# Cutting GpSimd's last store unevenly instead of SyncE's store of four earlier heads

## Chip, core and metric

The kernel runs on one core of one Trainium2 chip. The metric is the device time of one execution in microseconds (us), as the median of several runs.

## What is computed

Attention over 8 x 12 = 96 heads of 512 positions and 64 channels. The positions are the nodes of a binary tree in heap order, and a query sees only itself and its ancestors.

```python
mask = np.zeros((seq, seq))
for i in range(seq):
    mask[i, i] = 1
    parent = i
    while parent > 0:
        parent = (parent - 1) // 2
        mask[i, parent] = 1
scores = np.einsum('bhqd,bhkd->bhqk', Q, K) * scale
scores = scores + (1 - mask) * (-1e9)
weights = np.exp(scores - np.max(scores, axis=-1, keepdims=True))
weights = weights / (np.sum(weights, axis=-1, keepdims=True) + 1e-10)
return np.einsum('bhqk,bhkd->bhqd', weights, V).astype(np.float32)
```

## The kernel before

The 96 heads are worked in 48 pairs (NP = 48). The main loop runs over i = 0 to 48. Step i computes the scores of pair i on TensorE (`scores1`, `scores2`), takes their exponentials on ScalarE, multiplies the weights of pair i - 1 with V (`values`) and divides by the row sums on VectorE (`norm`, L691 and L693). `turn` transposes the keys and queries of later pairs. Loads of Q, K and V are issued from GpSimd, which converts them from f32 to bf16 on the way; GpSimd also copies pieces of V and of Q and K into place (L370, L444).

`norm` writes into output tiles `of` of eight heads each, 128 partitions x 8 heads x 256 floats. From pair 16 on, `head(i, a)` is 8 * (i // 4) + i % 4 + 4 * a: four pairs fill one tile, and pair i writes head x and head x + 4. So heads 76 and 77 are finished by pair 37, heads 78 and 79 by pair 39, heads 72 to 79 all by pair 39, and heads 80 to 87 by pair 43. Heads 88 to 95 are filled by the last four pairs.

`store(eng, h0, n, step, p0, p1)` (L700 to L706) writes n heads of one tile from the partitions p0 to p1 to the output. One head is 128 KB, 1 KB in each partition. An issue from GpSimd goes through the software queue (q0 in the profile), one from SyncE or ScalarE through a hardware queue (q1, q10). The order on GpSimd is a written list (`pool_program`, L717 to L763) whose operations are taken in order when `ready` allows; each then waits on chip for its data. Its stores are issued like this: heads 0 to 39 in the loop over loads, then 40 to 47, and so on by eight up to 80 to 87, with one exception: the store at 72 takes only four heads. The other four of that tile are stored by SyncE in `store_apart` (L711 to L715), called after step 41: heads 76 and 77 in two DMAs of partitions 0 to 59 and 60 to 127, heads 78 and 79 in one. SyncE stores 88 and 92, 89 and 93, 90 and 94 in pairs as they are finished (L890), then 91 (L892), and ScalarE stores 95 (L893).

The tiles are separate for each eight heads, and there are eleven buffers (NOUT // 2) for the twelve of them.

Of the kernel before, what the change touches and what calls it, by code (L numbers as in the profile page):

```python
# [119 lines left out]
def kernel(  # L120
# [7 lines left out]
    nc = tc.nc  # L128
    B, H, S, D = Q.shape
    P = nc.NUM_PARTITIONS  # L130
    assert S == 512 and D == 64 and P == 128 and (B * H) % 4 == 0
    scale = float(1.0 / np.sqrt(D))
    NH = B * H
# [3 lines left out]
    KB, VB = 8, 16  # L137
# [424 lines left out]
    def scores1(i):  # L562

        sp = psS.tile([P, 2, 512], fp32, name="s1")
        for a in range(2):
            nc.tensor.matmul(  # L566
                out=sp[:, a, :],
                lhsT=(k1code if i < WIDE else k1wide)[64 * a:64 * a + CODE_ROWS, :],
                rhs=(q1code, q1wide, q1far)[(i >= WIDE) + (i >= FAR)][64 * a:64 * a + CODE_ROWS],
                start=True, stop=False,  # L570
            )
        for a in range(2):
            nc.tensor.matmul(  # L573
                out=sp[:, a, :], lhsT=keys(i, a, TOP),
                rhs=qTs[i][64 * a:64 * a + 64, :, :].rearrange("p t c -> p (t c)"),
                start=False, stop=True,
            )
        et = etpool.tile([P, 2, 4, 128], bf16, name="e1")
        nc.scalar.activation(  # L579
            out=et[:, :, :, :].rearrange("p a t c -> p (a t c)"),  # L580
            in_=sp[:, :, :].rearrange("p a c -> p (a c)"),
            func=AF.Exp, scale=scale,
        ) if i < WIDE else nc.scalar.activation(  # L583
            out=et[:, :, :, :].rearrange("p a t (r u) -> p a (t r) u", u=2 if i < FAR else 4),
            in_=sp[:, :, :].rearrange("p a (u c) -> p a c u", u=2 if i < FAR else 4),
            func=AF.Exp, scale=scale,
        )
        ets[i] = et
# [34 lines left out]
    def scores2(i):  # L623
        if i >= WIDE:
            return scores2_wide(i)
        sp = psS.tile([P, 2, 4, 128], fp32, name="s2")
        flat = sp[:, :, :, :].rearrange("p a t c -> p a (t c)")
        for a in range(2):
            nc.tensor.matmul(
                out=sp[:, a, :, 32:128], lhsT=k2code[64 * a:64 * a + CODE_ROWS, :],  # L630
                rhs=q2code[64 * a:64 * a + CODE_ROWS, :].rearrange(
                    "p (t c) -> p t c", t=4
                )[:, :, 32:128],
                start=True, stop=False,
            )
        for t, lo, hi in ((2, 32, 192), (0, 192, 256), (3, 288, 448), (1, 448, 512)):
            for a in range(2):
                nc.tensor.matmul(
                    out=flat[:, a, lo:hi], lhsT=keys(i, a, TILE2[t]),
                    rhs=qTs[i][64 * a:64 * a + 64, :, :].rearrange("p t c -> p (t c)")[:, lo:hi],  # L640
                    start=False, stop=t == 1, skip_group_check=t in (2, 3),
                )
        nc.scalar.activation(
            out=e2s[i % NE][:, :, :, 32:128].rearrange("p a t c -> p (a t) c"),
            in_=sp[:, :, :, 32:128].rearrange("p a t c -> p (a t) c"),
            func=AF.Exp, scale=scale,
        )
# [52 lines left out]
    def store(eng, h0, n, step=1, p0=0, p1=P):  # L700
        return eng.dma_start(  # L701
            out=Or[p0:p1, h0:h0 + step * (n - 1) + 1:step, :],
            in_=ofs[h0 // 8][p0:p1, h0 % 8:h0 % 8 + step * (n - 1) + 1:step, :, :].rearrange(
                "p h t d -> p h (t d)"
            ),
        )  # L706


    APART, APART_AT, APART_ROWS = 76, 41, 60

    def store_apart():  # L711

        for p0, p1 in ((0, APART_ROWS), (APART_ROWS, P)):
            store(nc.sync, APART, 2, 1, p0, p1)
        store(nc.sync, APART + 2, 2)  # L715

    def pool_program():  # L717

        ops = [
            (load_k, 2, 2), (load_q, 2, 2), (load_v, 0, 4), (load_v, 4, 4),  # L720
            (load_k, 4, 2), (load_k, 6, 2), (load_q, 4, 2), (load_k, 8, 4),
            (load_q, 6, 2), (load_q, 8, 4), (load_v, 8, 8), (load_k, 12, 4),
            (load_q, 12, 4), (load_k, 16, 4), (load_rows, 1, "upper"),
            (load_q, 16, 4), (load_rows, 1, "even"), (load_k, 20, 4), (load_rows, 1, "odd"),
            (load_q, 20, 4), (load_k, 24, 8), (load_q, 24, 4), (load_rows, 2, "upper"),
            (load_q, 28, 4), (load_rows, 2, "leaves0", "leaves1"), (load_k, 32, 8), (load_q, 32, 8),
            (load_rows, 3, "upper"),
            (spread_pool, (1, "Z0", 8, 16), (1, "Z1", 8, 16), (1, 6, 8, 16), (1, 9, 8, 16)),
            (load_q, 40, 8), (load_k, 40, 8), (load_rows, 3, "leaves0", "leaves1"), (load_q, 48, 8),
            (spread_top, 2), (spread_pool, (2, "Z0", 0, 16), (2, "Z1", 0, 16)), (load_k, 48, 8),  # L730
            (spread_pool, (2, "X", 0, 16), (2, "M", 0, 16), (2, "D1", 0, 16)), (spread_top, 3, 0, 12),
            (load_rows, 4, "upper"), (spread_top, 3, 12, 16),
        ]
        loaded, stored = 72, 0
        for h in range(56, NH, KB):
            top = [(spread_top, h // VB + 0)] if h % VB == 8 and 4 <= h // VB + 0 < NH // VB else []
            if top:
                top.append((spread_pool, (h // VB, "Z0", 0, 16), (h // VB, "Z1", 0, 16)))
            ops += [(load_q, h, KB)] + top + [(load_k, h, KB)]
            if h == 64:  # L740
                ops.append((
                    spread_pool, *[(3, part, 0, 16) for part in ("Z0", "Z1", "X", "M", "D1")]
                ))
            while loaded < min(h + 32, NH):
                names = ("leaves0", "leaves1") if loaded % VB else ("upper",)
                ops.append((load_rows, loaded // VB) + names)
                loaded += KB
            if top:
                o = h // VB
                ops.append((spread_pool, *[(o, part, 0, 16) for part in ("X", "M", "D1")]))  # L750
            if stored + KB + BEHIND <= h + KB:
                ops.append((store, nc.gpsimd, stored, KB))
                stored += KB
        ops.append((lay_beside, "qst", 80 // KB))
        while stored < NH - KB:
            n = 4 if stored + 4 == APART else KB
            ops.append((store, nc.gpsimd, stored, n))
            if stored == 40:
                ops.append((lay_beside, "kst", 80 // KB))
            if stored == 64:  # L760
                ops += [(lay_beside, "qst", 88 // KB), (lay_beside, "kst", 88 // KB)]
            stored += KB
        return ops  # L763
# [58 lines left out]
    def spread_by(copy, table, steady, i):  # L822
# [7 lines left out]
        for args in todo:  # L830
            spread(copy, *args)

    program = pool_program()

    def pool(i):
# [21 lines left out]
    for i in range(NP + 1):  # L857
        steps = FIRST[i] if i < len(FIRST) else "SVK" if i % 2 else "SVQ"
        steps = "SQVK" if i == FAR - 1 else steps
        for step in steps:  # L860
            if step == "S" and i < NP:
                scores1(i)
                scores2(i)
            if step == "V" and i >= 1:
                values(i - 1)
                norm(i - 1)
                valued = True
            if step == "K" and kdone < NP:
                kdone = turn("kst", kdone)
            if step == "Q" and qdone < NP:  # L870
                qdone = turn("qst", qdone)
            if step == "W":
                nc.scalar.copy(
                    out=codes[64:64 + CODE_ROWS, 1280:1536], in_=codes[0:CODE_ROWS, 1280:1536]
                )
            if step == "X":
                spin("s1" if valued else "ob", 2)
            if step == "D":
                spread_by(nc.vector.tensor_copy, BY_VECTOR, STEADY_VECTOR, i)
            if step == "A":  # L880
                spread_by(nc.scalar.copy, BY_SCALAR, STEADY_SCALAR, i)
        if "D" not in steps:
            spread_by(nc.vector.tensor_copy, BY_VECTOR, STEADY_VECTOR, i)
        if "A" not in steps:
            spread_by(nc.scalar.copy, BY_SCALAR, STEADY_SCALAR, i)
        pool(i)
        if i == APART_AT:
            store_apart()
        if i >= NP - 3 and i < NP:
            store(nc.sync, head(i - 1, 0), 2, 4)  # L890
    assert not program
# [32 lines left out]
```

## Time and profile before

| | |
|---|---|
| runs | 133.47, 133.77, 133.95 us; median 133.77 |
| profiled execution, first to last instruction | 131.7 us |
| around that span, by the median | 2.07 us |
| granted TensorE clock, mean | 0.969 |
| busy: TensorE, VectorE, ScalarE, GpSimd | 113.8, 103.6, 101.0, 83.1 us |
| HBM read, written | 37.94 MB, 12.58 MB |
| GpSimd's store issues | 11, 9.9 us busy |

No time of the profiled execution apart from its span is given, so the span stands for it; the 2.07 us are what the runs' median has beyond it. Busy times are those of one execution. A DMA's time to landing goes from its issue to its last completion, so it holds the time that it stood in the queue. DMA shares are the time of all packets over that of 16 engines, and can exceed 1 where packets overlap.

### The profile page before, as it was taken

The page shows a single profiled execution, that of the slowest core. Times are in us where ns is not written, and L with a number is a line of the kernel's source. Part 1 is how long each engine was busy: PE and PEld are TensorE (multiplying, and loading weights), DVE is VectorE, ACT ScalarE, POOL GpSimd, SP SyncE. Part 2 cuts the span into 40 slices and gives each one's busy share as a digit, 9 for nine tenths or more (in the row PEclk, how much of TensorE's full clock was granted, in tenths as well). Part 3 has the DMA queues.
Part 4 walks back from the last instruction along what each step waited for, and adds up shares of the span by engine and source line. Part 5 has one row for each costly group of instructions (what it writes and reads, how often), then busy time and mean ns, then how long its engine had stood idle before and what let it go on. Part 6 is the DMA issues. An engine that isn't in the chain of part 4 may idle for free.

```text
span 131.7 us, 5422 instructions
## 1 busy us (share of the span) xinstructions
PE 113.8 (86%) x2350; PEld 79.8 (61%) x2353; DVE 103.6 (79%) x254; ACT 101.0 (77%) x163; POOL 83.1 (63%) x114
## 2 busy tenths in 40 slices
PE   6783999999899899999999998997998999999900
PEld 2341577676666567667676675765675777775600
DVE  3437849988999998989899879898899977975530
ACT  4357369979799997968997879895898878789800
POOL 6968734345493999895399899945999935002000
PEclk9999689999999999999999999999999999999975
DMA  2999999999999999999999999999999999999991
GB/s 98 239 181 194 198 198 200 202 202 206 204 200 212 205 203 208 211 205 204 207 207 201 301 275 204 285 290 234 339 218 332 241 288 402 402 398 392 397 350 64
DMA packets 28108, 32.25 MB, mean 245 GB/s; under 512 B 1165, under 2 KB 23309, under 8 KB 28085
## 3 DMA queue, kind: packets, MB, share of 16 engines
q0 software_dynamic: 25696, 29.63, 110.8%
q1 hardware_dynamic: 1829, 1.83, 3.9%
q10 hardware_dynamic: 560, 0.46, 1.2%
q8 instruction: 18, 0.29, 0.8%
q14 instruction: 5, 0.04, 0.1%
HBM read 37.94 MB, written 12.58 MB: 384 GB/s over the span
## 4 chain that ended last, share of the span: by engine, by line
DMA 30%; PE 30%; DVE 15%; POOL 9%; ACT 7%; issue 4%; ACTq 0%; POOLq 0%
DMA qst<-in_Q_dram 14%; DMA kst<-in_K_dram 11%; PE ob L661 10%; POOL vt L370 6%; DMA vst<-in_V_dram 5%; DVE of L693 5%; PE s L566 4%; DVE vt L370 3%; PE s L573 3%; ACT e L617 3%; PE s L600 2%; PE s L611 2%; ACT vt L370 2%; PE qtp L531 2%; PE ktp L469 2%
## 5 line engine op out<-in xcount | busy, mean ns | idle before, releaser
L583 ACT ACTIVATE e<-s 128x1024 bf16<-128x1024 f32 x40 | 40.9, 1022 | 13.0 <-PE s L573 12.7
L661 PE MATMUL ob<-vt,e 128*128 128x65 bf16 (+1 forms) x940 | 37.4, 198 | 1.5 <-DVE of L693 1.0
L661 PEld LDWEIGHTS <-e 128*128 128x128 bf16 (+1 forms) x960 | 30.5, 103 | 9.5 <-PE s L611 1.0
L370 POOL COPY vt<-vst 32x512 int32<-32x512 int32 (+4 forms) x44 | 32.6, 741 | 5.3 <-PE ob L661 3.1
L617 ACT ACTIVATE e<-s 128x384 bf16<-128x384 f32 x80 | 34.7, 490 | 0.0
L693 DVE TENSOR_TENSOR of<-ob,rec 128x512 f32<-128x512 f32 x47 | 32.5, 692 | 1.6
L370 DVE COPY vt<-vst 32x1024 bf16<-32x1024 bf16 (+5 forms) x47 | 21.4, 456 | 3.1 <-DMA vst<-in_V_dram 2.2
L691 DVE RECIPROCAL rec<-ob 128x8 f32<-128x8 f32 x47 | 9.6, 205 | 12.1 <-PE ob L661 11.2
L701 POOL DMA_DIRECT2D out_dram<-of x11 | 9.9, 898 | 8.9 <-DVE of L693 8.8
L573 PE MATMUL s<-qq,kq 64*128 64x512 bf16 x80 | 15.3, 377 | 0.0
L611 PE MATMUL s<-qq,kq 64*128 64x160 bf16 (+1 forms) x320 | 14.8, 208 | 0.3 <-issue 0.3
L611 PEld LDWEIGHTS <-kq 64*128 64x128 bf16 x320 | 12.3, 94 | 4.5 <-issue 0.5
L566 PE MATMUL s<-far,codes 40*128 40x512 bf16 x64 | 12.5, 386 | 0.1
L600 PEld LDWEIGHTS <-codes 40*128 40x128 bf16 x80 | 6.4, 95 | 10.1 <-issue 4.5
L579 ACT ACTIVATE e<-s 128x1024 bf16<-128x1024 f32 x8 | 8.2, 1022 | 5.2 <-PE s L573 5.2
L253 POOL DMA_DIRECT2D qst<-in_Q_dram x12 | 8.5, 708 | 5.5 <-DMA kst<-in_K_dram 3.1
L370 ACT COPY vt<-vst 32x512 int32<-32x512 int32 (+3 forms) x19 | 10.4, 545 | 2.1 <-DMA vst<-in_V_dram 1.6
L542 DVE COPY qq<-qtp 128x1024 bf16<-128x1024 bf16 x16 | 10.9, 682 | 0.8 <-PE qtp L537 0.8
L253 POOL DMA_DIRECT2D kst<-in_K_dram x11 | 8.4, 762 | 4.3 <-DMA vst<-in_V_dram 2.0
L600 PE MATMUL s<-far,codes 40*128 40x384 bf16 x64 | 10.6, 324 | 0.6 <-ACT e L617 0.5
L476 PE MATMUL ktp<-ptile,kst 128*64 128x128 bf16 x256 | 10.1, 220 | 0.9 <-DVE kq L493 0.3
L298 POOL DMA_DIRECT2D vst<-in_V_dram x7 | 5.6, 800 | 5.8 <-DMA vst<-in_V_dram 4.0
(56 smaller groups left out, 155.8 us busy)
## 6 DMA issues: line engine op xcount, KB each, us to landing
out_dram<-of POOLq DMA_DIRECT2D x10, 1024.0 KB, 15.7
kst<-in_K_dram POOLq DMA_DIRECT2D x9, 512.0 KB, 14.2
qst<-in_Q_dram POOLq DMA_DIRECT2D x8, 512.0 KB, 16.1
vst<-in_V_dram POOLq DMA_DIRECT2D x12, 256.0 KB, 13.2
vst<-in_V_dram POOLq DMA_DIRECT2D x6, 512.0 KB, 12.4
qst<-in_Q_dram POOLq DMA_DIRECT2D x6, 256.0 KB, 11.9
kst<-in_K_dram POOLq DMA_DIRECT2D x4, 256.0 KB, 9.6
out_dram<-of SPq DMA_DIRECT2D x4, 256.0 KB, 6.5
```

What stands on the lines that cost most here:

```text
L253: return nc.gpsimd.dma_start(out=kept[b][:, h0 % KB:h0 % KB + n, :, :].rearrange("p (g x) t d -> p g (x t d)", x=x), in_=src[:, h0 // x:(h ...
L370: return copy(out=dst, in_=src)
L476: nc.tensor.transpose(out=columns(kp[64 * a:64 * a + 64, :], mixed, *dims), in_=st[:, place[a], 4 * u + t, :], identity=ptile[:, 0:128],)
L542: nc.vector.tensor_copy(out=qqs[j][:, :, 8 * last:8 * last + 8, :].rearrange("p b u c -> p b (u c)"), in_=quarters,)
L566: nc.tensor.matmul(out=sp[:, a, :], lhsT=(k1code if i < WIDE else k1wide)[64 * a:64 * a + CODE_ROWS, :], rhs=(q1code, q1wide, q1far)[(i >= ...
L573: nc.tensor.matmul(out=sp[:, a, :], lhsT=keys(i, a, TOP), rhs=qTs[i][64 * a:64 * a + 64, :, :].rearrange("p t c -> p (t c)"), start=False, ...
L583: ) if i < WIDE else nc.scalar.activation(
L600: nc.tensor.matmul(out=flat[:, a, :, :].rearrange("p u (t c) -> p u t c", t=4)[:, :, :, 32 // n:], lhsT=k2wide[64 * a:64 * a + CODE_ROWS, ...
L611: nc.tensor.matmul(out=flat[:, a, :, lo:hi], lhsT=keys(i, a, WTILE2[t]), rhs=qT[64 * a:64 * a + 64, :, lo:hi], start=False, stop=t == 1, s ...
L617: nc.scalar.activation(out=e2s[i % NE][:, a, :, 32:128].rearrange("p t (r u) -> p t r u", u=n), in_=flat[:, a, :, :].rearrange("p u (t r) ...
L661: nc.tensor.matmul(out=ob[lo:hi, a, 65 * t:65 * t + 65], lhsT=e[:, a, PLACE[t], lo:hi], rhs=vt[vtile[tile_v][0]][:, head(i, a) % VB, vtile ...
L693: nc.vector.tensor_tensor(out=ofs[j][:, h0:h1 + 1:head(i, 1) - head(i, 0), :, :], in0=o4[:, a:a + n, :, 0:D], in1=rec[:, a:a + n, :, :].to ...
```

## The change

`store_apart` and its call are removed, and with them SyncE's DMAs for heads 76 to 79. The store at 72 loses its exception and takes all eight heads 72 to 79. The short description of the change says that heads 72 to 77 go in one DMA and heads 78 and 79 in two of 60 and 68 partitions. The code does this one tile later: its condition `stored + KB == NH - KB` is 80 + 8 == 96 - 8, so it is heads 80 to 85 that go in one DMA, and heads 86 and 87 in the two. In the built kernel GpSimd's last four DMAs are 128x8x256, 128x6x256, 60x2x256 and 68x2x256, the last three of one tile; before they ended with 128x4x256 and 128x8x256. GpSimd has two DMAs more, SyncE three fewer. The order on TensorE, VectorE and ScalarE is the same.

```diff
-    APART, APART_AT, APART_ROWS = 76, 41, 60
-
-    def store_apart():
-
-        for p0, p1 in ((0, APART_ROWS), (APART_ROWS, P)):
-            store(nc.sync, APART, 2, 1, p0, p1)
-        store(nc.sync, APART + 2, 2)
-
...
         while stored < NH - KB:
-            n = 4 if stored + 4 == APART else KB
-            ops.append((store, nc.gpsimd, stored, n))
+            if stored + KB == NH - KB:
+                ops.append((store, nc.gpsimd, stored, KB - 2))
+                for p0, p1 in ((0, 60), (60, P)):
+                    ops.append((store, nc.gpsimd, stored + KB - 2, 2, 1, p0, p1))
+            else:
+                ops.append((store, nc.gpsimd, stored, KB))
...
-        if i == APART_AT:
-            store_apart()
```

## The prediction

> **What bounds the kernel now.** I read the page's head and slices first, then busy time by windows over the last 22 us, then the DMA issues of that stretch one by one, then the waits at the end.
>
> ```profile
> span 131.7 us, 5422 instructions
> DMA  2999999999999999999999999999999999999991
> DMA 30%; PE 30%; DVE 15%; POOL 9%; ACT 7%; issue 4%; ACTq 0%; POOLq 0%
> ```
>
> The DMA engines are busy in every slice but the first and the last, and the chain that ended last spends as much in DMA as on TensorE. So the stores at the end do not run on an idle memory system: they stand in a backlog. The windows (columns: stretch, length, busy us of PE, PEld, DVE, ACT, POOL, granted clock, DMA share, GB/s) show that it lasts beyond the arithmetic:
>
> ```profile
> 110.00:114.00 4.00, 4.00 (x81) 2.95 (x79) 3.18 (x7) 3.22 (x6) 0.94 (x2) 1.00 1.04 400
> 114.00:118.00 4.00, 4.00 (x82) 3.04 (x76) 3.18 (x8) 3.23 (x7) 0.00 (x0) 1.00 1.03 400
> 118.00:122.00 4.00, 3.75 (x74) 2.45 (x70) 2.01 (x5) 3.83 (x7) 0.91 (x1) 1.00 1.01 394
> 122.00:126.00 4.00, 3.23 (x66) 2.16 (x62) 2.38 (x7) 2.75 (x6) 0.00 (x0) 1.00 1.00 384
> 126.00:130.00 4.00, 0.00 (x0) 0.00 (x0) 0.55 (x3) 0.00 (x0) 0.00 (x0) 0.63 0.74 264
> ```
>
> From 110 to 118 the DMA engines move 400 GB/s with a share over 1, and after 126, when TensorE has nothing left, they still move 4.00 us x 264 GB/s = 1.06 MB. At 400 GB/s that is 2.6 us. The store issues and their landings (KB, us from issue to landing) say what stands in that backlog; the timeline gives GpSimd's and SyncE's start times, the DMA view of a short window round each start gives the landing:
>
> ```profile
> 104.53 0.89 POOL L701 DMA_DIRECT2D out_dram<-of  x1
> out_dram<-of POOLq DMA_DIRECT2D x1, 1024.0 KB, 19.4
> 110.99 0.76 POOL L701 DMA_DIRECT2D out_dram<-of  x1 [0.82 <-DVE of L693]
> out_dram<-of POOLq DMA_DIRECT2D x1, 512.0 KB, 14.6
> 119.69 0.91 POOL L701 DMA_DIRECT2D out_dram<-of  x1 [7.94 <-DVE of L693]
> out_dram<-of POOLq DMA_DIRECT2D x1, 1024.0 KB, 8.7
> 121.54 0.39 SPq L701 DMA_DIRECT2D out_dram<-of  x1
> out_dram<-of SPq DMA_DIRECT2D x1, 256.0 KB, 7.1
> 125.27 1.14 SPq L701 DMA_DIRECT2D out_dram<-of  x2
> L701 SPq DMA_DIRECT2D out_dram<-of x7: 350/373/398, 106.4 to 126.1; - x7
> out_dram<-of SPq DMA_DIRECT2D x1, 128.0 KB, 4.2
> SPq L919 <- DMA out_dram<-of: 3.9, 5, 1.9
> ```
>
> GpSimd's store of 104.53 has landed whole at 123.9, that of 110.99 at 125.6, that of 119.69 (heads 80 to 87) at 128.4. SyncE's last store, the second of the pair that starts at 125.27, starts at 126.1 and lands at 130.3; at the end SyncE waits for stores (five waits, 3.9 us). So neither queue runs dry before about 128.4, and the kernel ends when the last of the 16 DMA engines has written its last row. The next row cuts 128.5 to 131 into 40 slices of 0.0625 us:
>
> ```profile
> GB/s 262 279 262 197 213 148 180 131 148 98 115 82 115 66 66 82 49 82 33 66 33 66 33 49 49 33 33 0 0 0 0 0 0 0 0 0 0 0 0 0
> ```
>
> The rate does not stop at once: it falls from 262 to 33 GB/s over 1.7 us. At 400 / 16 = 25 GB/s for one engine, about ten are still writing at 128.5 and one or two at 130.2. The engines are unevenly loaded and the slowest sets the end. What counts about this change is therefore not bytes in all, which stay the same, but bytes per DMA engine.
>
> **The change, part by part.** In the code the condition `stored + KB == NH - KB` holds at stored = 80. So GpSimd's store of heads 72 to 75 becomes one of all of 72 to 79, its store of 80 to 87 becomes one of 80 to 85, and heads 86 and 87 go in two DMAs of 60 and 68 partitions. SyncE's three DMAs for 76 to 79 go.
>
> *SyncE's three issues.* Removed, at
>
> ```profile
> 106.37 0.36 SPq L701 DMA_DIRECT2D out_dram<-of  x1
> 106.77 0.39 SPq L701 DMA_DIRECT2D out_dram<-of  x1
> 110.72 0.40 SPq L701 DMA_DIRECT2D out_dram<-of  x1
> SPq L701 <- DVE of L693: 11.7, 2, 10.4
> ```
>
> That is 1.15 us of a queue that then waits 10.4 us for VectorE: worth nothing. The bytes leave at 110.99 instead of 106.37 and 110.72, behind a software queue that is full until 123.9 anyway: nothing by itself.
>
> *GpSimd's two more issues.* One of its store issues takes
>
> ```profile
> L701 POOL DMA_DIRECT2D out_dram<-of x11: 763/912/962, 60.2 to 119.7; - x11
> ```
>
> so the 8-head store at 110.99 costs about 0.15 us more than the 4-head one, inside an idle 7.94 us. After 119.69 the six-head store and two small ones take at most 3 x 0.96 = 2.9 us: the last is queued by 122.6. The queue ahead of it is busy until 125.6, so 3 us of cover hide it. Without the cover it would cost up to 1.9 us. Nobody on GpSimd waits behind these.
>
> *Rows per engine.* This is the term with a price. How the hardware queue dealt the old uneven pair is seen in its packets (q1 is SyncE's, q0 GpSimd's; packets, MB, share), first in 116 to 117, then in 120 to 121:
>
> ```profile
> out_dram<-of SPq DMA_DIRECT2D x1, 120.0 KB, 7.4
> out_dram<-of SPq DMA_DIRECT2D x1, 136.0 KB
> out_dram<-of SPq DMA_DIRECT2D x1, 256.0 KB, 11.8
> q0 software_dynamic: 84, 0.31, 77.6%
> q1 hardware_dynamic: 85, 0.09, 24.6%
> q0 software_dynamic: 97, 0.38, 96.6%
> q1 hardware_dynamic: 21, 0.02, 6.0%
> ```
>
> In 116 to 117 the two queues alternate packet by packet (84 and 85). In 120 to 121 SyncE's queue moves a quarter of that, 21, until its 256 KB store lands at 122.5, 11.8 us after issue, where the next one took 7.1. A quarter of 16 engines is four: the 136 KB lay on four of them, 34 KB each, and held up what came behind. The 120 KB are 15 groups of four rows x 2 heads x 1 KB, 8 KB on an engine. So of the four heads 76, 77, 86 and 87, twelve engines wrote 8 + 16 = 24 KB and four wrote 58 KB. After the change 76 and 77 are even, 16 KB each; 86 and 87 are uneven in the software queue, which the trace of before never shows for such counts. At best 60 rows are 4 on each of 15 engines and 68 rows 5 on most, 18 KB in all. The twelve light engines then go from 24 to 34 KB: 10 KB at 25 GB/s, +0.41 us. The bounds of the light share are 16 KB before (+18 KB, 0.72 us) and 32 KB (+2 KB, 0.08 us); 24 is nearest to what the packets show. The four heavy ones lose 24 KB, 0.97 us.
>
> *Software packets for hardware ones.* 512 KB change queue. In 122.3 to 123.9 and 126 to 128:
>
> ```profile
> q0 software_dynamic: 171, 0.64, 101.3%
> q1 hardware_dynamic: 555, 0.54, 76.4%
> ```
>
> 1.6 us x 16 x 1.013 / 0.64 MB is 40.5 us per MB on an engine; 2 us x 16 x 0.764 / 0.54 MB is 45. The difference of 4.5 us per MB on 0.52 MB over 16 engines is 0.15 us of gain at most, 0 at least, since packet times overlap. I take 0.06, near the lower end.
>
> Sum: 0.41 - 0.06 = +0.35 us on the span of 131.7, which ends with SyncE's wait. The runs' median, 133.77, is 2.07 above that span and the rest does not change: 134.1 us, its own range 133.9 to 134.5.
>
> The Trainium skill (DMA: Bandwidth & Descriptors, "Why a DMA increments its semaphore by 16 and not by 1") deals a hardware DMA onto the largest count up to 16 that divides its partitions, 4 for 68: the quarter of packets agrees. For the software queue it reports rounding up for some copies, 5 rows for 68, an estimate of the same +10 KB, and otherwise the dividing count on consecutive engines, the second rival below.
>
> **The rivals.** *Only bytes count.* If the end followed the sum of bytes, the time would stay 133.77. For it: 400 GB/s whichever queue works. Against: the decay over 1.7 us. The same page ("Issuing engines are not separate DMA queues") says that all queues run on the same 16 engines and interleave; by that alone the result would be this one.
>
> *Four engines again, but late or slow ones.* If the software queue also lays 68 rows on four engines, and one of them is the last engine now, that one goes from 24 to 58 KB: 34 KB / 25 = +1.37 us, 135.1. It decides when the four include one that now ends after about 128.8; otherwise nothing changes. For it: the 136 KB row. Against: only a few engines still write at 130.
>
> *The heavy four set the end now.* Then they lose 0.97 us, until the light ones, 0.41 later than now, take over: the slope above leaves about 0.4 us, 133.4, faster. It decides if the last engine at 130.2 is one of the four; by number that is 4 of 16. Against: they were loaded at 112 to 122, and no row shows which engines were last.
>
> **How the numbers follow.** Chances: forecast 0.44, four late engines 0.28, heavy four 0.18, bytes 0.10. What a measurement tells from no change is 0.3%, 0.40 us. The forecast's size straddles it: 0.29 of its 0.44 lies above (a last engine that had less than 24 KB, or no packet gain), 0.15 below. Of the second case 0.25 lies above. So slower 0.29 + 0.25 = 0.54, same 0.15 + 0.03 + 0.10 = 0.28, faster 0.18. The range goes from the heavy four's 133.4 to 135.2, just over the late four's.
>
> **What would show it.** Right: POOL and TensorE rows up to 126 unchanged, no SyncE store before 121.5, the store of 80 to 85 and the small ones landing some 0.3 to 0.4 us after 128.4, and SyncE's last landing moved by as much. The late four would show as a longer thin tail at 25 to 100 GB/s and a 136 KB store that lands last. The heavy four would show as a tail that stops earlier and steeper. Wrong altogether would be a change before 110, a gap in q0 between 119 and 126, or an end that doesn't follow a store's landing.

## The result, and the profile after

The changed kernel takes 134.18 us (median of 22 runs, 133.54 to 135.37); in the same comparison the kernel before takes 133.58 (22 runs). The ratio is 1.0038, 95% interval 1.0020 to 1.0055: slower by 0.38%, about 0.5 us. The prediction was 134.1 us, +0.35, and slower.

The first profile after is of an execution with late arithmetic. Its head and its windows, to be set against the same windows of before:

```profile
span 133.4 us, 5419 instructions
...
PEclk9999999999999999999999997799998699999995
DMA  3999999999999999999999999999999999997982
```

```profile
114.00:118.00 4.00, 4.00 (x81) 3.03 (x77) 3.12 (x8) 3.22 (x7) 0.51 (x1) 1.00 1.03 403
118.00:122.00 4.00, 3.75 (x76) 2.66 (x70) 3.04 (x8) 3.61 (x7) 0.00 (x0) 1.00 1.00 388
122.00:126.00 4.00, 3.88 (x78) 2.52 (x75) 1.82 (x5) 3.80 (x7) 2.50 (x3) 1.00 0.82 307
126.00:130.00 4.00, 1.97 (x48) 1.44 (x41) 2.02 (x6) 1.41 (x3) 0.00 (x0) 0.94 0.87 271
```

The span is 1.7 us longer, but TensorE still works after 126, where it had finished before. In 122 to 126 the DMA engines move 307 GB/s instead of 384: the software queue has run low, since the stores of heads 80 to 87 come late. The timeline of GpSimd, of the first profile and then of a second one of the same kernel:

```profile
113.61 0.90 POOL L701 DMA_DIRECT2D out_dram<-of  x1 [3.30 <-DVE of L693]
122.31 2.50 POOL L701 DMA_DIRECT2D out_dram<-of  x3 [7.80 <-DVE of L693]
```

```profile
span 132.3 us, 5419 instructions
98.84 0.91 POOL L701 DMA_DIRECT2D out_dram<-of  x1
110.94 0.89 POOL L701 DMA_DIRECT2D out_dram<-of  x1 [0.20 <-issue]
119.63 2.50 POOL L701 DMA_DIRECT2D out_dram<-of  x3 [7.80 <-DVE of L693]
126.00 0.42 SPq L701 DMA_DIRECT2D out_dram<-of  x1
122.00:126.00 4.00, 3.17 (x64) 2.14 (x62) 2.43 (x7) 2.70 (x6) 0.13 (x1) 1.00 1.02 379
```

The last three stores of GpSimd start at 122.31 in one execution and at 119.63 in the other; in the kernel before it was 119.69. So the late arithmetic belongs to that one execution and not to the change. Its granted clock (row PEclk) fell to 0.7 and later to 0.6 before these stores, which is the likely reason. The second profile is the one to compare: arithmetic as before, DMA engines busy (379 GB/s), three issues in 2.50 us. Its landings (KB, us from issue to landing) of heads 80 to 85, of the 60 and of the 68 partitions of 86 and 87, and of SyncE's and ScalarE's last stores; then of the store of heads 32 to 39 (the row at 98.84), and the rate from 129 to 131.6 in 40 slices:

```profile
out_dram<-of POOLq DMA_DIRECT2D x1, 768.0 KB, 8.7
out_dram<-of POOLq DMA_DIRECT2D x1, 120.0 KB, 8.3
out_dram<-of POOLq DMA_DIRECT2D x1, 136.0 KB, 8.1
out_dram<-of SPq DMA_DIRECT2D x1, 128.0 KB, 4.6
out_dram<-of ACTq DMA_DIRECT2D x1, 128.0 KB, 4.4
out_dram<-of POOLq DMA_DIRECT2D x1, 1024.0 KB, 13.3
GB/s 142 158 110 126 79 110 79 110 63 79 79 63 47 47 47 47 47 47 47 47 47 47 47 47 0 0 0 0 0 0 0 0 0 0 0 0 0 0 0 0
```

SyncE's store of head 91 lands at 126.0 + 4.6 = 130.6, where before it was 130.3 (130.62 and 130.23 in the traces). But the store of heads 32 to 39, which the change does not touch, lands late as well, at 112.18 where before it was 111.86. So 0.32 of these 0.39 us were there before the change could act.

### The profile page after: what moved, and what is told of

It reads as the page before. It is cut to its first block, busy times and chain, and to the rows that moved or that the text cites. A ratio compares the mean times of both kernels' runs of the same rounds, so it can differ in the third digit from the quotient of the medians.

```text
span 133.4 us, 5419 instructions
## 1 busy us (share of the span) xinstructions
PE 116.2 (87%) x2350; PEld 81.3 (61%) x2353; DVE 103.5 (78%) x254; ACT 101.1 (76%) x163; POOL 85.5 (64%) x116
## 2 busy tenths in 40 slices
DMA packets 27833, 32.25 MB, mean 242 GB/s; under 512 B 1272, under 2 KB 22904, under 8 KB 27810
## 4 chain that ended last, share of the span: by engine, by line
DMA 32%; PE 28%; POOL 17%; DVE 10%; ACT 5%; issue 4%; ACTq 0%; POOLq 0%
DMA qst<-in_Q_dram 14%; DMA kst<-in_K_dram 11%; POOL vt L370 9%; PE ob L661 9%; DMA vst<-in_V_dram 7%; PE s L566 4%; DVE of L693 3%; DVE vt L370 3%; PE s L573 3%; ACT e L617 3%; POOL kst L243 2%; PE s L600 2%; POOL qst L243 2%; PE s L611 2%; PE qtp L531 2%
## 5 line engine op out<-in xcount | busy, mean ns | idle before, releaser
L370 POOL COPY vt<-vst 32x512 int32<-32x512 int32 (+4 forms) x44 | 33.1, 752 | 5.5 <-PE ob L661 3.3
L701 POOL DMA_DIRECT2D out_dram<-of x13 | 11.5, 888 | 11.1 <-DVE of L693 11.1
L573 PE MATMUL s<-qq,kq 64*128 64x512 bf16 x80 | 15.8, 390 | 0.0
L611 PE MATMUL s<-qq,kq 64*128 64x160 bf16 (+1 forms) x320 | 15.3, 212 | 0.1
L537 PE MATMUL qtp<-ptile,qst 128*64 128x128 bf16 x192 | 7.6, 223 | 2.6 <-DMA qst<-in_Q_dram 2.6
```

The lines of the kernel that those rows point to most:

```text
L370: return copy(out=dst, in_=src)
L573: nc.tensor.matmul(out=sp[:, a, :], lhsT=keys(i, a, TOP), rhs=qTs[i][64 * a:64 * a + 64, :, :].rearrange("p t c -> p (t c)"), start=False, ...
L611: nc.tensor.matmul(out=flat[:, a, :, lo:hi], lhsT=keys(i, a, WTILE2[t]), rhs=qT[64 * a:64 * a + 64, :, lo:hi], start=False, stop=t == 1, s ...
L701: return eng.dma_start(out=Or[p0:p1, h0:h0 + step * (n - 1) + 1:step, :], in_=ofs[h0 // 8][p0:p1, h0 % 8:h0 % 8 + step * (n - 1) + 1:step, ...
```

## The experiments

Each was timed beside the kernel before on the same chip; the ratios are to that kernel. The first four, the next four and the last four ran together, each four on another chip, with medians of the kernel before of 133.96, 134.09 and 133.54 us. So ratios are compared here, and not times.

**The changed kernel again** (no edit).

> The changed kernel once more, unaltered, for a second profile and more times. Theory A (rows per DMA engine: the software queue lays the 68 rows on four engines, which set the end): about 0.5 us over the kernel before, and a thin tail of four engines at the end of the profile. Rival B (software instead of hardware queue for 512 KB): also 0.5 us over, but without a thin tail. Rival C (the arithmetic ends later, as in the first profile after, where GpSimd's last large store starts at 122.3 instead of 119.7): the store of heads 80 to 85 starts again about 2.6 us later than before.

Measured: 134.28 us, ratio 1.0020 (0.9991 to 1.0050). The arithmetic is not later (rival C falls, above). The number alone would not tell +0.2% from nothing; with the first comparison it fits +0.4%. The tail above ends at 47 GB/s, which is two engines at 25 GB/s each and not the four of theory A.

**Nothing uneven.** GpSimd stores heads 80 to 87 whole, since the condition never holds.

```diff
-            if stored + KB == NH - KB:
+            if stored < 0:
```

> GpSimd stores heads 80 to 87 whole: nothing in the kernel is uneven any more, and all of 72 to 87 goes through the software queue. Theory A: the four heavy engines lose 26 KB, 1.0 us, and the others gain 8 KB, 0.3 us: between the two kernels or below, 133.5 to 133.9. Rival B: as slow as the changed kernel, 134.1. Rival C: as slow as the changed kernel.

Measured: 134.51 us, ratio 1.0037 (1.0010 to 1.0063). It is not faster than the changed kernel. So four heavy engines are not what costs time: taking their load away did not help, and dealing evenly costs 0.5 us against the kernel before.

**The same on SyncE**, in the kernel before.

```diff
-        for p0, p1 in ((0, APART_ROWS), (APART_ROWS, P)):
-            store(nc.sync, APART, 2, 1, p0, p1)
+        store(nc.sync, APART, 2)
```

> The kernel before, with SyncE's heads 76 and 77 in one DMA of 128 partitions instead of 60 and 68. Theory A: twelve engines go from 24 to 32 KB of these heads (+0.3 us) and four from 58 to 32 (-1.0 us): 133.9 if light engines set the end before, 133.2 if the heavy four did. Rival B: as the kernel before, 133.6, since the queue is the same.

Measured: 134.44 us, ratio 1.0022 (1.0000 to 1.0044). The queue is that of before and the time is not: the unevenness itself was worth some 0.3 us, though the interval begins at no difference. Here theory A has its light engines right, and its heavy ones wrong.

**A second uneven pair** in the changed kernel.

```diff
-                ops.append((store, nc.gpsimd, stored, KB - 2))
-                for p0, p1 in ((0, 60), (60, P)):
-                    ops.append((store, nc.gpsimd, stored + KB - 2, 2, 1, p0, p1))
+                ops.append((store, nc.gpsimd, stored, KB - 4))
+                for h in (stored + KB - 4, stored + KB - 2):
+                    for p0, p1 in ((0, 60), (60, P)):
+                        ops.append((store, nc.gpsimd, h, 2, 1, p0, p1))
```

> The changed kernel with a second uneven pair: heads 84 and 85 also in two DMAs of 60 and 68 partitions on GpSimd. Theory A: four more engines, or the same ones, get 34 KB: 0.3 to 1.4 us over the changed kernel, 134.4 to 135.5, and a longer thin tail. Rival B: as the changed kernel, 134.1, plus nothing, since the bytes of each queue are the same.

Measured: 134.13 us, ratio 0.9999 (0.9968 to 1.0029). The expected loss did not come. Theory A was given up here, and theory D formed: a few engines are late whatever this pair does, and every byte that the uneven dealing keeps from them shortens the end. How many they are can be read from the last slices of the kernel with everything even, 129 to 131.6 in 40 slices:

```profile
GB/s 221 126 173 95 142 63 95 32 63 32 63 32 63 47 47 32 63 47 47 47 47 63 32 47 47 47 0 0 0 0 0 0 0 0 0 0 0 0 0 0
```

For the last 1.2 us the rate is about 48 GB/s, which at 25 GB/s each is two engines. The trace also has the times of the 16 completions of a store, taken here as one for each engine. Of SyncE's last store here fourteen come by 129.50 and two at 130.80 and 130.84; of the store of heads 32 to 39 the last is at 111.69 and the fourteenth at 111.56. So two engines fall 1.3 us behind in between. In the kernel before it is 0.5 us (129.65, then 130.15 and 130.23).

**The uneven pair of 86 and 87 from SyncE** instead of GpSimd.

```diff
-                for p0, p1 in ((0, 60), (60, P)):
-                    ops.append((store, nc.gpsimd, stored + KB - 2, 2, 1, p0, p1))
...
+        if i == 44:
+            for p0, p1 in ((0, 60), (60, P)):
+                store(nc.sync, 86, 2, 1, p0, p1)
```

> The changed kernel with the uneven pair of heads 86 and 87 (60 and 68 partitions) issued from SyncE instead of GpSimd; GpSimd stores 80 to 85. Theory D (two slow DMA engines end the kernel, and what they are dealt of the uneven pair decides; the hardware queue spares them more than the software queue): as the kernel before, 0.2 to 0.5 us under the changed kernel, since the hardware queue deals the pair as it did 76 and 77. Rival E (it counts that the uneven pair is early and beside the software queue): as the changed kernel or slower, since the pair now comes last.

Measured: 134.08 us, ratio 1.0009 (0.9991 to 1.0027). As near to the kernel before as it can be told, with heads and place of the changed kernel. By the ratio itself that takes back most of the loss, though its interval still reaches the changed kernel's lower end. Nothing speaks for rival E.

**Halves.**

```diff
-                for p0, p1 in ((0, 60), (60, P)):
+                for p0, p1 in ((0, 64), (64, P)):
```

> The changed kernel with heads 86 and 87 cut into 64 and 64 partitions instead of 60 and 68. The number of DMAs stays, every engine gets the same. Theory D: as the kernel with the whole store, 0.5 to 0.65 us over the kernel before. Rival F (more and smaller DMAs of GpSimd are what helped or hurt): as the changed kernel, 0.3 to 0.4 us over the kernel before.

Measured: 134.43 us, ratio 1.0029 (1.0009 to 1.0049), 0.39 us. That is within rival F's range and a tenth under theory D's, and the interval holds both: the time does not decide here. This kernel and the changed one have the same number of DMAs and differ in rows alone, so their packet counts tell how the software queue deals. The rows of the DMA view, of the changed kernel, of the halves and of the second uneven pair:

```profile
DMA packets 27833, 32.25 MB, mean 242 GB/s; under 512 B 1272, under 2 KB 22904, under 8 KB 27810
```

```profile
DMA packets 27721, 32.25 MB, mean 244 GB/s; under 512 B 1162, under 2 KB 22794, under 8 KB 27698
```

```profile
DMA packets 27977, 32.25 MB, mean 244 GB/s; under 512 B 1414, under 2 KB 23046, under 8 KB 27954
```

60 and 68 partitions instead of 64 and 64 bring 1272 - 1162 = 110 packets under 512 B. If 68 rows lie on four engines, each has 34 KB, that is 8 packets of 4 KB and one of 2 KB; if 60 rows lie on 15, each has 2 packets of 4 KB. With one tiny packet in place of each of these on every engine that gets no rows, that makes 12 x 9 + 1 x 2 = 110. The sizes in the trace agree: 98 packets of 16 B and 12 of 8 B, of which the halves have none, and four more of 2 KB, one for each heavy engine. The second pair adds 110 once more and 32 completions of its two DMAs: 1272 + 142 = 1414, as counted. Rounding up would leave three engines without rows and at most 8 such packets. The dealing of the second rival of the prediction is the one that happens.

**120 and 8 partitions** of 76 and 77 on SyncE, in the kernel before (`APART_ROWS` 120).

```diff
-    APART, APART_AT, APART_ROWS = 76, 41, 60
+    APART, APART_AT, APART_ROWS = 76, 41, 120
```

> The kernel before, with SyncE's heads 76 and 77 cut into 120 and 8 partitions instead of 60 and 68. Taking the dealing rule of the Trainium skill (DMA: Bandwidth & Descriptors, on how many engines a DMA uses), 120 rows lie on engines 0 to 14 and 8 rows on 0 to 7: engine 15 gets nothing of the pair, as before, engines 8 to 14 get 16 KB and 4 to 7 get 18 KB instead of 8, and 0 to 3 get 18 instead of 42. Theory D15 (both slow engines gain nothing here, or engine 15 alone sets the end): 0 to 0.1 us over the kernel before. Theory D-other (one of the two slow ones is among 4 to 14): +0.3 to +0.4 us, and a tail of one engine, about 25 GB/s, instead of two. Rival (the heavy four set the end): faster by up to 0.9 us.

Measured: 134.45 us, ratio 1.0017 (0.9998 to 1.0037). Not faster: the heavy four do not set the end. Between the two forms of D the number does not decide; it lies between them. The last slices, 128.5 to 131.5, lack the sign of D-other, a tail of one engine:

```profile
GB/s 191 232 123 205 191 219 137 205 177 164 82 109 96 96 82 109 82 68 68 82 41 41 55 55 41 41 55 55 41 41 55 55 0 0 0 0 0 0 0 0
```

It is two engines to the end, and their completions of SyncE's last store come at 130.95 and 130.97. So D-other lacks its sign and the number lies above D15's; which engines are the late ones stays open.

**119 and 9 partitions** there (`APART_ROWS` 119).

```diff
-    APART, APART_AT, APART_ROWS = 76, 41, 60
+    APART, APART_AT, APART_ROWS = 76, 41, 119
```

> The kernel before, with SyncE's heads 76 and 77 cut into 119 and 9 partitions. By the same dealing rule, 119 rows lie 17 each on engines 0 to 6 and 9 rows on 0 to 8: engines 0 to 6 get 36 KB, 7 and 8 get 2 KB, 9 to 15 nothing, instead of 42 for 0 to 3, 8 for 4 to 14 and 0 for 15. Theory D with a slow engine among 7 to 14 and engine 15: that one is 0.25 to 0.3 us earlier, engine 15 as before, so 0 to 0.1 us under the kernel before. With both slow engines among 7 to 14: 0.25 to 0.3 us under it. With a slow engine among 4 to 6: 1.1 us over it.

Measured: 133.76 us, ratio 0.9978 (0.9958 to 0.9997). The completions show the dealing (one more of each store comes at its issue): seven for the 119 rows, at 118.8 to 120.1, and nine for the 9 rows, of which two come at 113.4 and seven at 119.4 to 120.7, right behind those of the 119. So the same seven engines wrote 34 + 2 KB. Moving the rows to so few engines was not slower but here 0.3 us faster; it lies 0.4% under the 120 and 8. This fits theory D with a late engine among those that get 2 KB or nothing.

**119 and 9 from GpSimd**, for heads 86 and 87 of the changed kernel, and **the same in the other order**.

```diff
-                for p0, p1 in ((0, 60), (60, P)):
+                for p0, p1 in ((0, 119), (119, P)):
```

> The changed kernel with heads 86 and 87 cut into 119 and 9 partitions instead of 60 and 68. Theory G (the software queue lays a DMA on as many engines as the dividing count says, one after another from a place that moves on: 119 rows on seven engines, 34 KB each, and 9 rows on the next nine, 2 KB each, and since 7 + 9 = 16 on the same ones in each execution): if the place begins at engine 0, the slow engines get 2 KB and the kernel is as fast as the 119 and 9 on SyncE, 0.1 to 0.3 us under the kernel before. Rival H (the software queue rounds up, 8 rows on each of 15 engines): 18 KB on nearly all, as the whole store, 0.4 to 0.5 us over the kernel before.

```diff
-                for p0, p1 in ((0, 60), (60, P)):
+                for p0, p1 in ((119, P), (0, 119)):
```

> The same with the order turned: the 9 partitions first, then the 119. Theory G: now the nine engines from the place on get 2 KB and the next seven 34 KB; with the place at engine 0 those are 9 to 15 and hold a slow one, so it gets 18 KB more than in the whole store: 0.7 us over that, 1.0 to 1.2 us over the kernel before. Rival H: no difference to the other order.

Measured: 134.07 us, ratio 1.0030 (1.0000 to 1.0060), and 134.56 us, 1.0072 (1.0048 to 1.0097). The packet counts are the same for both; of the first:

```profile
DMA packets 27817, 32.25 MB, mean 244 GB/s; under 512 B 1250, under 2 KB 22882, under 8 KB 27794
```

1250 - 1162 = 88, and 119 rows on seven engines (9 packets) with 9 rows on nine (one packet) give 9 x 9 + 7 x 1 = 88. So how many engines get rows is as theory G says, and rival H falls. With equal bytes, packets and DMAs the order alone moves the ratio by 0.4%, and the other order is the slowest kernel of all; nine of the twelve runs of the first order are below the fastest of the other. That the first order would be faster than the kernel before failed. Its runs spread from 133.38 to 135.27, while nine of the twelve of the other order lie in 134.39 to 134.71; but without its slowest run it spreads from 133.38 to 134.44, and the kernel before, without its two slowest, from 133.19 to 134.60, so the spread alone shows little. Where the software queue begins stays open. The last slices of the other order, 128.5 to 131.5:

```profile
GB/s 205 191 341 478 314 369 342 137 123 205 150 219 123 150 191 150 109 123 109 96 82 82 68 55 41 41 55 55 41 41 55 55 41 55 41 55 41 27 27 27
```

Two engines again, now to 131.2, and one beyond.

Which engines got the rows can be read from the trace in this execution. Each heavy share, of 119 rows or of 68, ends with a packet of 2 KB. Here the last two of the seven shares of the 119 rows end at 129.26 and 129.68, and the last two completions of that store follow at 129.85 and 130.16, 1.3 us behind the others: both late engines had 34 KB of it. In the second profile of the changed kernel the four shares of the 68 rows end by 127.49. The last two completions follow at 129.18 and 129.28 behind tiny packets that end at 128.69 and 128.80: there both late engines had none of these rows.

**9 first on SyncE**, and **both of SyncE's pairs uneven** (76 and 77 as 119 and 9, 78 and 79 as 120 and 8), each in the kernel with `APART_ROWS` 119.

```diff
-        for p0, p1 in ((0, APART_ROWS), (APART_ROWS, P)):
+        for p0, p1 in ((APART_ROWS, P), (0, APART_ROWS)):
```

> The kernel with 119 and 9 partitions of heads 76 and 77 on SyncE, with the 9 first. The hardware queue begins at engine 0 for each DMA, so theory D (what the slow engines are dealt decides): as with the 119 first, 0.1 to 0.4 us under the kernel before. If the order mattered on SyncE as theory G has it for GpSimd: 0.5 us or more over the kernel before.

```diff
-        store(nc.sync, APART + 2, 2)
+        for p0, p1 in ((0, 120), (120, P)):
+            store(nc.sync, APART + 2, 2, 1, p0, p1)
```

> The kernel before with heads 76 and 77 on SyncE as 119 and 9 partitions, and heads 78 and 79 as 120 and 8. Beside the 119 and 9 alone, engine 15 loses 16 KB and engines 0 to 7 gain 2. If engine 15 sets the end there: 0.3 to 0.6 us faster than with the 119 and 9 alone, so 0.5 to 0.9 us under the kernel before. If one of the other slow engines or one of the first seven does: +0.1 us, 0.1 to 0.2 us under the kernel before.

Measured: 133.69 us, ratio 0.9999 (0.9970 to 1.0029), and 133.51 us, 0.9991 (0.9963 to 1.0019). On SyncE the other order brings no loss like that on GpSimd. The gain of 119 and 9 is not seen again, nor a further one; no version here is shown to beat the kernel before. One reason is in the profile of the 9 first, GpSimd's store of heads 32 to 39, SyncE's last store and its landing:

```profile
99.47 0.91 POOL L701 DMA_DIRECT2D out_dram<-of  x1
128.10 0.35 SPq L701 DMA_DIRECT2D out_dram<-of  x1
out_dram<-of SPq DMA_DIRECT2D x1, 128.0 KB, 1.8
```

The arithmetic came late here (SyncE's last store at 128.1 instead of 126.1), and the store landed in 1.8 us instead of 4.2: in such an execution no engine has a backlog left, and relieving one brings nothing.

A measure inside the profiles helps to read the times. GpSimd's store of heads 32 to 39 and SyncE's last store bracket the stretch in which the engines work off the backlog. Their starts and landings, for the kernel before, for the whole store and for the 9 first on GpSimd:

```profile
98.89 0.92 POOL L701 DMA_DIRECT2D out_dram<-of  x1
out_dram<-of POOLq DMA_DIRECT2D x1, 1024.0 KB, 13.0
```

```profile
98.79 0.91 POOL L701 DMA_DIRECT2D out_dram<-of  x1
out_dram<-of POOLq DMA_DIRECT2D x1, 1024.0 KB, 12.9
125.95 0.35 SPq L701 DMA_DIRECT2D out_dram<-of  x1
out_dram<-of SPq DMA_DIRECT2D x1, 128.0 KB, 4.9
```

```profile
100.03 0.91 POOL L701 DMA_DIRECT2D out_dram<-of  x1
out_dram<-of POOLq DMA_DIRECT2D x1, 1024.0 KB, 11.9
127.23 0.35 SPq L701 DMA_DIRECT2D out_dram<-of  x1
out_dram<-of SPq DMA_DIRECT2D x1, 128.0 KB, 4.6
```

From landing to landing it is 130.3 - 111.9 = 18.4 us before, 130.85 - 111.7 = 19.15 with everything even, and 131.8 - 111.9 = 19.9 with the 9 first. At 25 GB/s the first step, 0.75 us, is about 19 KB and the second, another 0.75, the same: near the 16 KB that the even dealing gives an engine that got nothing of 76 and 77, and the 18 KB between 16 and 34. The arithmetic of the 9 first is 1.2 us late, but its late engines still had GpSimd's rows to write when SyncE's last store was issued. The other traces, one execution each, by the issue of SyncE's last store:

| kernel | issue, us | from landing to landing, us |
|---|---|---|
| changed kernel, second profile | 126.0 | 18.4 |
| 119 and 9 from GpSimd | 126.2 | 18.8 |
| uneven pair of 86 and 87 from SyncE | 126.3 | 18.4 |
| the same (nothing uneven) on SyncE | 126.6 | 19.1 |
| 120 and 8 on SyncE | 126.6 | 18.6 |
| second uneven pair | 126.8 | 19.5 |
| halves | 126.8 | 19.0 |
| 119 and 9 on SyncE | 127.6 | 18.6 |
| 9 first on SyncE | 128.1 | 18.6 |
| changed kernel, first profile | 128.7 | 20.0 |
| both of SyncE's pairs uneven | 129.3 | 19.4 |

All three kernels that deal evenly have 19 us or more. But the changed kernel's second profile is at 18.4, as before: in that execution, in which the late engines were spared, the stretch shows no loss. And the second uneven pair is at 19.5 though its median is that of the kernel before, so one execution does not stand for a kernel.

## Why the prediction was right, point by point

*The end is set by the last of 16 engines in a backlog.* Held. Equal bytes gave ratios of 0.9978 to 1.0072, and in eight of the fourteen traces the last half microsecond or more belongs to two engines, in two more to one. "Only bytes count" falls with the two orders of 119 and 9.

*SyncE's issues and GpSimd's two more are worth nothing.* Held in the profile with the same arithmetic: 2.50 us for three issues, the store of 80 to 85 landing at 128.3 (119.63 + 8.7) as the store of 80 to 87 had at 128.4. The cover assumed for them was thin in the first profile after, where the arithmetic was late and the queue low.

*Rows per engine.* The reading of the kernel before held: SyncE's 68 rows complete on four engines (at 118.9 to 119.3) and its 60 on fifteen, so, if both stores begin at the same engine as the 119 and 9 did, one of the twelve light engines had 16 KB and not 24. The sign and the size of the change came out (+0.35 in sum, 0.5 measured), but the step "at best 60 rows are 4 on each of 15 engines and 68 rows 5 on most" failed: the software queue lays 68 rows on four engines, as the packet counts show. So the +10 KB on twelve engines did not happen: an engine outside the four has 16 + 8 = 24 KB after the change as before. The number came out by luck. What the runs show in its place is that two late engines end the kernel, and that the time follows what they are dealt: taking SyncE's uneven pair away costs 0.2%, and an even dealing by GpSimd 0.3 to 0.4%. The changed kernel's uneven pair, dealt by GpSimd, does not give that back in the median, though in one traced execution the late engines had none of its 68 rows and the stretch was as short as before. Whether its four engines change from one execution to the next, and how often they hold a late one, is not shown; that this makes the 0.4% is argued and stays open.

*The heavy four set the end.* Fell: of the three kernels that took load from them (1.0037, 1.0022, 1.0017) none was faster.

*Four engines again, late ones.* Its dealing is right; its price of 1.37 us on top was seen only in part, as the 0.75 us between even and the 9 first on GpSimd, where it is counted from 16 KB and not 24. In the changed kernel's second profile the late engines were not among the four.

*Software for hardware packets, 0.06 us.* Too small for these intervals: even by GpSimd 1.0037, even on SyncE 1.0022, and the intervals overlap widely.

The page DMA: Bandwidth & Descriptors of the Trainium skill ("Why a DMA increments its semaphore by 16 and not by 1") has both ways of dealing; the counts agree with its dividing rule, 4 for 68 and 7 for 119, on the software queue too, and none of these uneven stores was rounded up. Its advice not to cut a transfer into two partition halves ("Rules for kernel authors") agrees with the halves: 1.0029, no better than the whole store.

## What to carry to other kernels

In a tail that is bound by DMA, count bytes per DMA engine and not in all: an edit that moves no byte in sum can cost half a microsecond (ratio 1.0037 with everything even), by the estimate above if the latest engines get some 16 KB more. A partition count such as 60, 68 or 119 is an instrument for that, and its effect depends on the issuing queue: on a hardware queue the order of two uneven DMAs made no difference that could be seen, on the software queue 0.4%. Before an explanation is built on a single profile after, see whether the arithmetic in it came at the same time, and whether what the change does not touch landed at the same time too.

## What was not expected of the hardware

An engine that gets no rows of a software-queue DMA gets tiny packets in the number of the others' packets: 110 and 88 more, each matched exactly by that count, of 16 B beside packets of 4 KB and of 8 B beside those of 2 KB. And two of the 16 engines end last by 1.0 to 1.7 us in the traces of the three kernels that deal all the same bytes of these stores. In the last microsecond their packets take no longer than the others' (46 ns for 1 KB), so the delay arose earlier. Which two, and why, no run shows; nor why both end together with 120 and 8, where at most one of them can have had none of the pair.
